# Scores of the latent queries: the product of query hi and key lo over 64 rows, two query tiles on two halves of TensorE's rows

## The chip, the cores and the metric

The kernel runs on one NeuronCore of one Trainium2 chip. The metric is the time of one execution on the device, in microseconds (us), as the median of several runs. TensorE does the matrix products into PSUM, VectorE (DVE), ScalarE (ACT) and GpSimd (POOL) do the rest, and SyncE issues the transfers (DMA).

## What is computed

Two layers of a diffusion block over 256 latent tokens and 256 context tokens of width 1024. Each layer normalises and modulates its input, projects it once, and runs three mixers on it: A, global attention; B, pooling; C, attention in a band of 128 tokens with a sink. A and C have 6 query heads and 2 key heads of 64 channels. The three are gated, summed and projected, and a squared-ReLU MLP follows. The part that the change touches is the scores, in the reference's words (A; C adds a mask and a sink):

```python
def one_block(qi):                       # 128 queries
    sc = jnp.einsum('bqhgd,bkhd->bhgqk', qi, k).astype(jnp.float32) * scale
    p = jax.nn.softmax(sc, axis=-1).astype(v.dtype)
    return jnp.einsum('bhgqk,bkhd->bqhgd', p, v)
```

Latent queries attend to the 256 context keys and 256 latent keys. Context queries attend to context keys alone, and only layer 0 needs them.

## The kernel before, in words

**Precision.** TensorE multiplies in a rounded fp32 format (fp32r). To keep fp32 accuracy each operand is split into a rounded part, hi, and the remainder, lo, and a product is the sum of three: hi·hi, hi·lo and lo·hi (`mm3`, line 439).

**Scores.** A head has only 64 channels, half of TensorE's 128 rows. So the query tile `q` (`Q`, lines 1162 to 1197) holds hi in one half of the rows and lo in the other: `Q.tile` writes hi and lo of each head side by side into a staging tile `stk` (line 1175), and `Q.finish` transposes it (TensorE, `qT`) and copies it to `q`. The keys (`KV`, lines 1113 to 1160) are staged twice over, so that `kh` holds key hi in both halves and `kl` holds key lo in both halves. `attend_unit` (lines 1208 to 1309) works on one head and one stream `s` (0 latents, 1 context), with two query tiles of 128. Per query tile it issues, over all 128 rows, `q` times `kh` (hi·hi + lo·hi) and `q` times `kl` (hi·lo + lo·lo). For latents (`lat`) each product has 512 columns (keys) and each query tile a PSUM bank of its own; in branch C a product of the identity and a mask, 128 columns, follows in the same bank. For context the products have 256 columns, and both query tiles share a bank. Then come the row maximum of each tile (VectorE, `mx`, line 1244), the exponential (ScalarE, `p`), the normalisation, the transposes of the probabilities (TensorE, `pT`), their split into hi and lo (`pth`, `ptl`) and the products with the values (`po`).

**Order.** All work is written as generators ("threads") with priorities, and `_Flow.run` (line 268) plays them against a simple model of the engines while the program is built: the thread that is ready in the model, with the lowest priority number, goes next. `_TensorEngine._step` (line 148) books 0.0022 us and one cycle for each column of a product, whatever its rows, and marks its output as ready 0.2 us later. Each engine then runs its instructions in the order that results. Attention units run as lanes (`attend_lane`, 2 per branch in layer 0, 3 in layer 1), and the projection, gate and branch products of the layer fill TensorE between their steps.

**A product with few rows elsewhere.** At the start `First.end` (line 546) turns rows of the modulation into columns with products over 4 rows of plain fp32 (`adat`, line 557), four per block, which appear as eight records each.

Of the kernel before, what the change touches and what calls it, by code (L numbers as in the profile page):

```python
# [15 lines left out]
P = 128  # L16
# [4 lines left out]
HD = 64  # L21
# [155 lines left out]
class _Flow:  # L177
# [58 lines left out]
    def free(self, *aps):  # L236

        for name in {ap.tensor.name for ap in aps}:
            self.shares[name] -= 1
            if self.shares[name]:  # L240
                continue
            p = self.pools[self.owner.pop(name)]
            p[0] -= 1
            p[1].append(self.uses[name] + 0.1)
# [48 lines left out]
P_NORM, P_ATT, P_SPLIT, P_SIDE, P_ADA, P_MAIN = range(6)  # L293
# [3 lines left out]
def kernel(ctx: ExitStack, tc: tile.TileContext, a: dict, out: bass.AP):  # L297
    nc = tc.nc
    ctx.enter_context(tc.manual_schedule())
    fl = _Flow()  # L300
# [3 lines left out]
    PE = _TensorEngine(fl, nc.tensor)  # L304
# [21 lines left out]
    def half(dt=F32, s="h"):  # L326
        t = bp.tile([P, 256], dt, tag="h", name=nm(s), bufs=T_BUFS)
        fl.take("h", t)
        return t

    def small(w, s="s", bufs=12):
        return sp.tile([P, w], F32, tag=s, name=nm(s), bufs=bufs)

    def bank(s="ps"):
        t = pp.tile([P, 512], F32, tag="ps", name=nm(s))
        fl.take("ps", t)
        return t
# [4 lines left out]
    def const(shape, dt, s):  # L342
        return cp.tile(shape, dt, tag=s, name=s)
# [367 lines left out]
    identr = const([P, P], F32R, "identr")  # L711
# [12 lines left out]
    mask = const([P, 2, P], F32R, "mask")  # L724
# [18 lines left out]
    def rms_scale(ss, n, width):  # L743

        V.tensor_scalar(out=ss, in0=ss, scalar1=1.0 / width, scalar2=EPS, op0=ALU.mult, op1=ALU.add)
        yield fl.ready(ss)
        G.tensor_tensor(out=ss, in0=ss, in1=neg_half[:, :n], op=ALU.pow)
# [159 lines left out]
    def layer(l, hT, hT_next):  # L907
# [35 lines left out]
        rsq = {br: cp.tile([P, 4, NH], F32, tag=f"rsq{br}", name=f"rsq{br}_{l}") for br in "AC"}  # L943

        def qk_norm(ps, c0, nh, kind, t, hi, lo, ev, rs=None):


            w = nh * HD
            src = ps[:, c0 : c0 + w]
            yield tabs_ev  # L950
            yield fl.ready(src)
            yield from fl.room("h", 2, T_BUFS)
            yield from S.calm(SIDE_CALM[l])
            sq = half(s="sq")
            rv = small(4, "qr")[:, :nh] if rs is None else rs
            if QR_ACT[l]:
                for i in range(nh):
                    S.activation(sq[:, i * HD : (i + 1) * HD], src[:, i * HD : (i + 1) * HD], AF.Square, accum_out=rv[:, i : i + 1])
            else:
                S.activation(sq[:, :w], src, AF.Square)  # L960
                yield fl.ready(sq[:, :w])
                V.tensor_reduce(out=rv, in_=sq[:, :w].rearrange("p (h d) -> p h d", h=nh), axis=AX.X, op=ALU.add)
            free(sq)
            zv = src.rearrange("p (h d) -> p h d", h=nh)
            z = None
            if rs is None:
                yield fl.ready(rv)
                yield from rms_scale(rv, nh, HD)
                yield fl.ready(rv)
                yield from fl.room("h", 1, T_BUFS)  # L970
                z = half(s="z")
                zn = z[:, :w].rearrange("p (h d) -> p h d", h=nh)
                V.tensor_tensor(out=zn, in0=zv, in1=rv.unsqueeze(2).to_broadcast([P, nh, HD]), op=ALU.mult)
                zv = zn
                yield fl.ready(z[:, :w])
            yield from fl.room("h", 3, T_BUFS)
            yield from V.calm(SIDE_CALM[l])
            y = half(s="y")
            yv = y[:, :w].rearrange("p (h d) -> p h d", h=nh)
            if t >= 2:  # L980
                V.tensor_tensor(out=yv, in0=zv, in1=gains[:, l, kind].unsqueeze(1).to_broadcast([P, nh, HD]), op=ALU.mult)
            else:
                y2 = y[:, :w].rearrange("p (h d e) -> p h d e", h=nh, e=2)
                ms = []
                for e in range(2):
                    m = half(s="m")
                    mv = m[:, :w].rearrange("p (h d) -> p h d", h=nh)
                    V.tensor_tensor(out=mv, in0=zv, in1=tabs[kind][:, e, t].unsqueeze(1).to_broadcast([P, nh, HD]), op=ALU.mult)
                    ms.append(m)
                yield fl.ready(*[m[:, :w] for m in ms])  # L990
                yield from V.calm(SIDE_CALM[l])
                for e in range(2):
                    m2 = ms[e][:, :w].rearrange("p (h d e) -> p h d e", h=nh, e=2)
                    V.tensor_tensor(out=y2[:, :, :, e], in0=m2[:, :, :, 0], in1=m2[:, :, :, 1], op=ALU.add)
                free(*ms)
            if z is not None:
                free(z)
            yield fl.ready(y[:, :w])
            if len(hi.shape) == 4:
                yv = yv.unsqueeze(2).to_broadcast([P, nh, 2, HD])  # L1000
            S.copy(out=hi.bitcast(F32R), in_=yv)
            yield fl.ready(hi)
            V.tensor_tensor(out=lo, in0=yv, in1=hi, op=ALU.subtract)
            free(y)
            fl.set(ev, lo)
            if rs is not None:
                V.tensor_scalar(out=rs, in0=rs, scalar1=HD * EPS, scalar2=None, op0=ALU.add)
                yield fl.ready(rs)
                G.tensor_tensor(out=rs, in0=rs, in1=neg_half[:, :nh], op=ALU.pow)
            done_with(ps)  # L1010
# [3 lines left out]
        def done_with(ps):  # L1014

            n = ps.tensor.name
            readers[n] -= 1
            if readers[n] == 0:
                free(ps)

        def reads(ps):
            readers[ps.tensor.name] = readers.get(ps.tensor.name, 0) + 1
# [90 lines left out]
        class KV:  # L1113
# [15 lines left out]
            def tile(self, t, ps):  # L1129
                st = tmp(s="stk").rearrange("p (h a e d) -> p h a e d", h=NKV, a=2, e=2)  # L1130
                self.sts.append(st)
                self.wait.append(_Event())
                reads(ps)
                reads(ps)
                fl.spawn(qk_norm(ps, 0, NKV, self.kind, t, st[:, :, 0], st[:, :, 1], self.wait[-1]), P_SIDE)
                fl.spawn(self.split_v(ps, t), P_SIDE)
# [25 lines left out]
        class Q:  # L1162
# [5 lines left out]
            def tile(self, t, ps):  # L1168
                st = tmp(s="stk").rearrange("p (h e d) -> p h e d", h=4, e=2)
                self.sts.append(st)  # L1170
                for c0, nh, kind, br, h0 in self.segs:
                    s = st[:, c0 // HD : c0 // HD + nh]
                    self.wait.append(_Event())
                    reads(ps)
                    fl.spawn(qk_norm(ps, c0, nh, kind, t, s[:, :, 0], s[:, :, 1], self.wait[-1], rsq[br][:, t, h0 : h0 + nh]), P_SIDE)

            def close(self):
                fl.spawn(self.finish(), P_SIDE)
# [29 lines left out]
        def attend_unit(br, h, s):  # L1208
# [5 lines left out]
            kh, kl = kkt[br, kv]  # L1214
            q = qst[br, h]
            lat = s == 0
            k0, nk = (0, 512) if lat else (256, 256)
            nb = nk // P
            mx = small(2, "mx")
            sc_ = []  # L1220
# [3 lines left out]
            for i in range(2):  # L1224
                qt = 2 * s + i
                qs = q[:, qt * P : (qt + 1) * P]
                sc = bank("sc") if lat else sc_bank[:, i * 256 : i * 256 + 256]
                masked = br == "C" and lat
                PE.matmul(sc[:, :nk], qs, kh[:, k0:], start=True, stop=False)
                PE.matmul(sc[:, :nk], qs, kl[:, k0:], start=False, stop=not masked)  # L1230
                if masked:
                    kb = 1 - qt
                    PE.matmul(sc[:, kb * P : (kb + 1) * P], identr, mask[:, qt], start=False, stop=True)
                sc_.append(sc)
            left[br, "q", h] -= 1
            if left[br, "q", h] == 0:
                free(q)
# [97 lines left out]
        def attend_lane(br, units):  # L1335
            for h, s in units:
                yield from attend_unit(br, h, s)
# [479 lines left out]
        for blk in range(nblk):  # L1817
# [63 lines left out]
            if blk == 0 and not last:  # L1881
# [3 lines left out]
                for j in range(2):  # L1885
                    w = ws.next()
                    w2_.append(w)
                    for i in range(2):
                        yield from banks()
                        ps = bank("h1")  # L1890
# [7 lines left out]
            if last:  # L1898
# [5 lines left out]
                for t in range(2):  # L1904
                    for j in range(2):
                        yield from banks()
                        ps = bank("h1")
# [11 lines left out]
            while c < nc1:  # L1919
                w = ws.next()  # L1920
                for i in range(2):
                    yield from banks()
                    ps = bank("h1")
# [46 lines left out]
    h0 = Normed()  # L1970
# [144 lines left out]
```

## Time and profile before

| what | us |
|---|---|
| median of 3 runs | 1152.64 |
| lowest and highest | 1149.83, 1153.02 |
| the profiled execution | 1151.59 |
| its span, first to last instruction | 1149.8 |
| its mean granted TensorE clock | 0.996 of 2.4 GHz |

How to read the rows further down: PE is TensorE's products, PEld its weight loads, which are instructions of their own in front of each product and run beside the product ahead. DVE is VectorE. `sc<-kk,q 128*128 128x512` is the product that writes `sc` from `kk` and `q`, with 128 rows by 128 columns of weights, and 128 x 512 of the other operand. L170 and L174 are the helper lines through which all products and transposes pass. Products are pipelined: the duration of one reaches from its start to the modelled end of its results, so products overlap in the timeline, and what one costs in a dense stream is the distance of the starts. A line that ends with a bracket tells of idle time before it and who ended it; "issue" there means that the engine waited for nothing that the profile shows.

### The profile page before, as it was taken

Reading aid. Unit: us, or ns where it says so; the run is one execution under the profiler, and the core shown is the slowest. Engines: PE = TensorE matmul, PEld = TensorE weight load, DVE = VectorE, ACT = ScalarE, POOL = GpSimd, SP = SyncE. Lnnn points to the kernel's source line nnn. Section 1 sums busy time; section 2 is a strip of 40 time slices with the busy share of each in tenths; the row PEclk is TensorE's granted clock in tenths of the full one; section 3 lists DMA queues with packets and bytes.
Section 4 is the critical chain, followed back from the end, with each engine's and each line's share of the span. In section 5 each row is a group of like instructions: output and inputs, shape, how many; then the busy total and the mean of one; then the engine's idle time right before and its main releaser. Section 6 shows DMA issues by size and latency. Waiting matters only on the chain.

```text
span 1149.8 us, 16635 instructions
## 1 busy us (share of the span) xinstructions
PE 1126.2 (98%) x5984; PEld 957.4 (83%) x5984; DVE 884.0 (77%) x1653; ACT 650.3 (57%) x1372; POOL 60.6 (5%) x76
## 2 busy tenths in 40 slices
PE   5999999999999999999999999999999999999998
PEld 2788888888888898888888888888888888999886
DVE  6889887899899679888676734679777886987453
ACT  7867668667653574422133423576878855765432
POOL 0123002000000100000000000012020000000000
PEclk9999999999999999999999999999999999999999
DMA  8742332353454335455555633555324570775662
GB/s 319 272 158 92 110 123 74 126 165 119 165 164 154 126 124 192 154 195 174 200 199 186 206 105 109 166 171 183 92 82 159 182 256 19 267 243 183 192 215 75
DMA packets 59987, 186.77 MB, mean 162 GB/s; under 512 B 7296, under 2 KB 8064, under 8 KB 59904
## 3 DMA queue, kind: packets, MB, share of 16 engines
q1 hardware_dynamic: 59904, 185.71, 48.7%
q8 instruction: 47, 0.77, 0.3%
q14 instruction: 36, 0.29, 0.1%
HBM read 184.63 MB, written 1.05 MB: 161 GB/s over the span
## 4 chain that ended last, share of the span: by engine, by line
PE 87%; DVE 6%; ACT 4%; DMA 2%; issue 1%; SPq 0%; POOL 0%; DVEq 0%; ACTq 0%
PE tm L170 28%; PE h L170 22%; PE g L170 15%; PE qkv L170 5%; PE br L170 4%; PE po L170 2%; PE sc L170 2%; PE pT L174 2%; DMA ad<-in_wada_dram 1%; PE u L170 1%; ACT hh L136 1%; PE ada L170 1%; PE xT L174 1%; ACT p L136 1%; DVE wl L136 1%
## 5 line engine op out<-in xcount | busy, mean ns | idle before, releaser
L136 DVE TENSOR_TENSOR wl<-st,wh 128x1024 fp32r<-128x1024 f32 x216 | 263.4, 1221 | 125.2 <-ACT wh L136 124.9
L136 ACT CAST wh<-st 128x1024 fp32r<-128x1024 f32 x216 | 227.8, 1058 | 223.5 <-PE tm L170 139.9
L170 PE MATMUL h<-hh,wh 128*128 128x256 f32 (+1 forms) x736 | 186.6, 316 | 0.0
L170 PE MATMUL h<-hh,wl 128*128 128x256 f32 (+1 forms) x512 | 168.8, 330 | 0.9 <-DVE wl L136 0.9
L136 DVE SCALAR_TENSOR_TENSOR acc<-sta,s_col,acc 128x512 f32<-128x512 f32 x224 | 159.3, 745 | 2.2 <-DMA sta<-in_wada_dram 1.8
L170 PE MATMUL tm<-wh,ah 128*128 128x512 f32 x384 | 149.9, 390 | 0.0
L170 PE MATMUL tm<-wl,ah 128*128 128x512 f32 x384 | 149.5, 389 | 0.0
L170 PE MATMUL tm<-wh,al 128*128 128x512 f32 x384 | 149.4, 389 | 0.0
L170 PEld LDWEIGHTS h<-hh,wh 128*128 128x128 f32 x736 | 124.3, 191 | 8.7
L170 PE MATMUL h<-hl,wh 128*128 128x512 f32 (+1 forms) x288 | 105.5, 366 | 0.1
L170 PEld LDWEIGHTS h<-hh,wl 128*128 128x128 f32 x512 | 97.3, 190 | 10.0 <-DVE wl L136 1.1
L170 PEld LDWEIGHTS tm<-wh,al 128*128 128x128 f32 x384 | 72.1, 188 | 15.2
L170 PEld LDWEIGHTS tm<-wl,ah 128*128 128x128 f32 x384 | 72.1, 188 | 14.9
L170 PEld LDWEIGHTS tm<-wh,ah 128*128 128x128 f32 x384 | 72.1, 188 | 14.6
L170 PE MATMUL g<-hh,wh 128*128 128x512 f32 x192 | 76.7, 400 | 0.0
L170 PE MATMUL g<-hh,wl 128*128 128x512 f32 x192 | 75.0, 391 | 0.0
L170 PE MATMUL g<-hl,wh 128*128 128x512 f32 x192 | 75.0, 391 | 0.0
L136 ACT ACTIVATE relu<-h 128x512 f32<-128x512 f32 (+1 forms) x64 | 31.0, 487 | 65.9 <-PE h L170 65.6
L170 PE MATMUL qkv<-wh,hh 128*128 128x256 f32 (+1 forms) x192 | 65.3, 340 | 1.1 <-ACT hh L136 1.1
L170 PE MATMUL qkv<-wl,hh 128*128 128x256 f32 (+1 forms) x192 | 64.3, 335 | 1.8 <-DVE wl L136 1.8
L170 PE MATMUL qkv<-wh,hl 128*128 128x256 f32 (+1 forms) x192 | 64.0, 333 | 0.0
L170 PEld LDWEIGHTS h<-hl,wh 128*128 128x128 f32 x288 | 54.3, 189 | 9.2 <-DVE hl L136 0.5
(207 smaller groups left out, 2230.9 us busy)
## 6 DMA issues: line engine op xcount, KB each, us to landing
st<-in_w_dram SPq DMA_DIRECT2D x136, 512.0 KB, 4.4
sta<-in_wada_dram SPq DMA_DIRECT2D x80, 512.0 KB, 4.0
st<-in_win_dram SPq DMA_DIRECT2D x48, 512.0 KB, 4.3
st<-in_wing_dram SPq DMA_DIRECT2D x24, 512.0 KB, 4.2
ad<-in_wada_dram SPq DMA_DIRECT2D x32, 256.0 KB, 6.1
st<-in_wout_dram SPq DMA_DIRECT2D x8, 512.0 KB, 4.7
wor<-in_wout_dram SPq DMA_DIRECT2D x16, 256.0 KB, 6.1
grow<-in_b_ada_dram SPq DMA_DIRECT2D x12, 256.0 KB, 5.5
```

What stands on the lines that cost most here:

```text
L136: return fn(*args, **kw)
L170: return self._e.matmul(out, lhsT, rhs, start=start, stop=stop)
L174: return self._e.transpose(out, in_, identity)
```

## The change

For latent units the two `q` times `kl` products over 128 rows are replaced. Now the two `kh` products (and in branch C the masks) of both query tiles come first, and then two products over 64 rows each: for query tile 0 the upper half of the rows, for query tile 1 the lower half, both of 512 columns, each into its tile's own bank. They hold hi·lo only, so lo·lo is no longer added. So that hi lies in the right half, `Q.tile` swaps hi and lo in the staging tile for odd query tiles. Context units keep their four products.

```diff
--- before.py
+++ after.py
@@ -1172,7 +1172,8 @@
                     s = st[:, c0 // HD : c0 // HD + nh]
                     self.wait.append(_Event())
                     reads(ps)
-                    fl.spawn(qk_norm(ps, c0, nh, kind, t, s[:, :, 0], s[:, :, 1], self.wait[-1], rsq[br][:, t, h0 : h0 + nh]), P_SIDE)
+
+                    fl.spawn(qk_norm(ps, c0, nh, kind, t, s[:, :, t % 2], s[:, :, 1 - t % 2], self.wait[-1], rsq[br][:, t, h0 : h0 + nh]), P_SIDE)
 
             def close(self):
                 fl.spawn(self.finish(), P_SIDE)
@@ -1227,11 +1228,16 @@
                 sc = bank("sc") if lat else sc_bank[:, i * 256 : i * 256 + 256]
                 masked = br == "C" and lat
                 PE.matmul(sc[:, :nk], qs, kh[:, k0:], start=True, stop=False)
-                PE.matmul(sc[:, :nk], qs, kl[:, k0:], start=False, stop=not masked)
+                if not lat:
+                    PE.matmul(sc[:, :nk], qs, kl[:, k0:], start=False, stop=True)
                 if masked:
                     kb = 1 - qt
-                    PE.matmul(sc[:, kb * P : (kb + 1) * P], identr, mask[:, qt], start=False, stop=True)
+                    PE.matmul(sc[:, kb * P : (kb + 1) * P], identr, mask[:, qt], start=False, stop=False)
                 sc_.append(sc)
+            if lat:
+                for i in range(2):
+                    r = slice(i * HD, i * HD + HD)
+                    PE.matmul(sc_[i], q[r, i * P : (i + 1) * P], kl[r], start=False, stop=True)
             left[br, "q", h] -= 1
             if left[br, "q", h] == 0:
                 free(q)
```

## Rows read from the trace of the kernel before

**Rows 1.** Page, busy us of each engine, share of the span.

```profile
PE 1126.2 (98%) x5984; PEld 957.4 (83%) x5984; DVE 884.0 (77%) x1653; ACT 650.3 (57%) x1372; POOL 60.6 (5%) x76
```

**Rows 2.** Page, the chain of work that ended last, by engine.

```profile
PE 87%; DVE 6%; ACT 4%; DMA 2%; issue 1%; SPq 0%; POOL 0%; DVEq 0%; ACTq 0%
```

**Rows 3.** Windows view: us, busy and count, granted clock; both attention stretches.

```profile
100.00:350.00 250.00, 249.42 (x1304) 211.66 (x1303) 220.68 (x452) 165.78 (x390) 10.39 (x9) 1.00 0.40 131
800.00:912.00 112.00, 109.64 (x612) 93.55 (x611) 89.47 (x198) 89.55 (x210) 6.21 (x6) 1.00 0.41 132
```

**Rows 4.** Waits of TensorE: us in total, times, longest.

```profile
PE po L170 <- DVE ptl L136: 0.9, 2, 0.7
...
PE pT L174 <- ACT p L136: 0.6, 2, 0.3
...
PE po L170 <- ACT p L136: 0.3, 1, 0.3
...
PE g L170 <- DVE wl L136: 0.2, 1, 0.2
```

**Rows 5.** Groups by form, score products: busy us, mean ns, idle before.

```profile
L170 PE MATMUL sc<-kk,q 128*128 128x512 f32 x96 | 27.7, 404 | 0.0
...
L170 PE MATMUL sc<-mask,identr 128*128 128x128 f32 x24 | 5.3, 221 | 0.0
```

**Rows 6.** Timeline, TensorE products, a steady stretch: start, us, what, [idle before].

```profile
274.80 0.39 PE L170 MATMUL br<-oh,kl 128*128 128x512 f32 x1
275.03 0.39 PE L170 MATMUL g<-hh,wh 128*128 128x512 f32 x1
275.25 0.39 PE L170 MATMUL g<-hl,wh 128*128 128x512 f32 x1
275.48 0.39 PE L170 MATMUL g<-hh,wl 128*128 128x512 f32 x1
```

**Rows 7.** Timeline, weight loads of the same stretch.

```profile
275.03 0.19 PEld L170 LDWEIGHTS g<-hl,wh 128*128 128x128 f32 x1
275.26 0.19 PEld L170 LDWEIGHTS g<-hh,wl 128*128 128x128 f32 x1
```

**Rows 8.** Timeline, products and loads at the start of one 4-row block.

```profile
45.82 0.60 PE L174 MATMUL xT<-ident,xh 128*128 128x128 f32 x4
...
46.35 0.18 PEld L170 LDWEIGHTS adat<-pair_sum,arow 4*128 4x128 f32 x1 [0.17 <-issue]
```

**Rows 9.** Timeline, the same at the start of another block.

```profile
44.14 0.28 PE L170 MATMUL qkv<-wh,hl 128*128 128x256 f32 x1
...
44.35 0.18 PEld L170 LDWEIGHTS adat<-pair_sum,arow 4*128 4x128 f32 x1
```

**Rows 10.** Timeline, products and loads at the end of the first block.

```profile
46.93 0.47 PE L170 MATMUL adat<-pair_sum,arow 4*128 4x2 f32 x3
...
47.33 0.19 PEld L170 LDWEIGHTS qkv<-wh,hh 128*128 128x128 f32 x1
```

**Rows 11.** Timeline, the same at the end of the other block.

```profile
44.93 0.47 PE L170 MATMUL adat<-pair_sum,arow 4*128 4x2 f32 x3
...
45.33 0.20 PEld L174 LDWEIGHTS xT<-ident,xh 128*128 128x128 f32 x2
```

**Rows 12.** Timeline, the loads of the whole first block.

```profile
46.35 0.96 PEld L170 LDWEIGHTS adat<-pair_sum,arow 4*128 4x128 f32 x8 [0.17 <-issue]
```

**Rows 13.** Timeline, the last product of a latent unit of branch C.

```profile
270.42 0.22 PE L170 MATMUL sc<-mask,identr 128*128 128x128 f32 x1
```

**Rows 14.** Waits of VectorE, the row maxima: us, times, longest.

```profile
DVE mx L136 <- PE sc L170: 20.5, 17, 4.1
```

**Rows 15.** Timeline, the weight load behind the product of rows 13.

```profile
270.42 0.14 PEld L174 LDWEIGHTS pT<-ident,p 128*128 128x128 f32 x1
```

## The prediction

> **What bounds the kernel now.** I read the page's busy shares first, then its chain of work, then the stretches in which the attention runs, then single instructions around the products that change. TensorE is busy for 1126.2 of 1149.8 us and holds 87% of the chain that ended last [rows 1, 2]. In the two attention stretches it is busy for 249.4 of 250 and 109.6 of 112 us, at a granted clock of 1.00 (2.4 GHz), while VectorE has 29 and 22 us to spare [rows 3]. All that TensorE waits for in the attention's own products, and in the gate products run among them, is a few waits of under 1 us in sum each [rows 4]. So the end moves with the time that TensorE's instruction stream takes, and with hardly anything else. One run beside another can tell 0.3% (3.5 us) from no change.
>
> **What the change touches.** There are 96 score products of 512 columns [rows 5]: 24 latent units (2 layers, 2 branches, 6 heads), four each. In each unit the two "query times key lo" products over 128 rows go, and two over 64 rows come, one on the upper and one on the lower half of the rows, one behind the other at the end of the unit. The swap of the halves for odd query tiles only alters which half of a staging tile is written: the same two instructions per tile, no cost. The mask products of branch C stay, ahead of the new pair. No DMA, no other instruction and no queue changes.
>
> **Price of a product as it is.** A 512-column product shows 0.39 us, but starts follow each other by 0.23 us (274.80, 275.03, 275.25, 275.48) [rows 6], since the weights of the next are loaded while one streams: each load starts with the product before its own [rows 7]. So the pair costs 2 × 0.23 = 0.46 us now. Laid fully over each other, two products would cost 0.23: a gain of 0.23 us a unit, 24 × 0.23 = 5.5 us. That is all that can be gained.
>
> **Price of changing the row mode.** The trace has one kind of product that doesn't fill the rows: the 4-row products of the modulation's start (adat), in blocks of eight records. At both edges of a block the overlap of load and product is gone. Before one block the last 128-row product ends at 45.82 + 0.60 = 46.42, and the first 4-row load starts at 46.35, 0.07 us before that end, with 0.17 us of idleness put down to "issue", so to no wait that the profile shows [rows 8]; another block is entered alike (44.14 + 0.28 = 44.42, load at 44.35) [rows 9]. On the way out it is the same: 46.93 + 0.47 = 47.40 and 44.93 + 0.47 = 45.40, with loads at 47.33 and 45.33 [rows 10, 11]. Inside a block loads follow each other by (0.96 - 0.19) / 7 = 0.11 us [rows 12], so there the load is not held. I read this as: a load of another row mode starts only 0.07 us before the modelled end of the product ahead, and its product streams 0.11 us later.
>
> The Trainium skill, "TensorEngine Tiling (Array Packing)", Key Properties, says that changing the tiling mode, though not the tile, drains TensorE. By that rule, the trace agrees at these four edges with its 0.07 us; a 64-row edge is in no row here.
>
> *Entry.* In branch A the product ahead is one of 512 columns (0.39 us), starting at S. The load starts at S + 0.32, its product streams at S + 0.43 instead of S + 0.23: 0.20 us lost. In branch C it is a mask product (0.22 us) [rows 13], after which the next product is held by its own load to S + 0.11 anyway: now S + 0.15 + 0.11 = S + 0.26, so 0.15 us lost. *Exit.* The second 64-row product is one of 512 columns: 0.20 us lost, whatever follows. Bounds: a gain is not excluded if half-array modes cost no drain (0 per switch); above, nothing in the rows is dearer than 0.20.
>
> *The pair itself.* Below: both loads run together and both products stream together, gain 0.23. Above: the products don't overlap, gain 0. Between: the second load follows the first by 0.11 us as in the 4-row block, and its product streams 0.11 us behind the first, gain 0.23 - 0.11 = 0.12. I take the last, because the 4-row loads are the nearest row, though they all use the same rows of the array.
>
> The same skill, "TensorE: Matmul & The Clock Gate", Part 3, gives about 4 ns between the starts of packed products on different row groups; no row here shows such a pair. By it the gain would be 0.23 us, and the sum worked out below 3.5 us instead of 6.1.
>
> **What follows on the other engines.** The first row maximum of a unit now waits for the fourth or sixth product instead of the second or third. Counted from the start of the second hi product: before, the first lo product ended at 0.39 - 0.23 = 0.16; now the pair's first ends at 0.43 + 0.39 = 0.82, 0.66 us later, while TensorE's own next work is 0.28 later. Queued behind the maximum on VectorE are weight splits and modulation sums. That is up to 0.38 × 24 = 9.1 us more of waiting, on an engine with 51 us to spare in these stretches, besides the 20.5 us which the maxima wait already [rows 3, 14]. I cost it at nothing: the order written by the planner books both lo products ahead of the maximum (2 × 0.2155 us by its own price), so it already moves the transposes back by most of that. If that cover is gone, TensorE stalls at the probability transposes. The planner's new order may also change the waits of these stretches, of which TensorE has 0.6 + 2.4 us now: I allow ±2 us.
>
> **The sum.** Branch A: 0.20 + 0.20 - 0.12 = 0.28 us a unit; branch C: 0.15 + 0.20 - 0.12 = 0.23. Twelve units each: 3.4 + 2.8, about 6.1 us longer. The profiled execution took 1151.59 us, so 1157.7; the median shown is 1.05 above it, which would give 1158.7. I put the forecast between them, at 1158.
>
> **Rivals.**
> - *Half modes cost no drain* (faster). The four edges [rows 8 to 11] are of products of plain fp32 and a quarter of the rows, and the drain may belong to that. Against: the transposes are declared fp32 too, and their load starts with the product ahead (270.42 on both engines) [rows 13, 15]. The edge at the unit's end decides: below about 0.12 us per switch (half of 0.23) the change gains. With none, 24 × 0.23 = 5.5 us go: 1146 to 1147. Chance 0.24.
> - *Drain, but loads and products wholly together.* Branch A 0.40 - 0.23 = 0.17, branch C 0.12: 12 × 0.29 = 3.5 us, 1155 to 1156, at the edge of what is told from no change. This is the case of the Trainium skill's page on the clock gate, cited above. Chance 0.16.
> - *Drain and no overlap: the change doesn't do what it says.* 0.40 and 0.35: 9.0 us, about 1161. For it: every product in the trace streams after the one ahead. Chance 0.13.
> - *Stalls at the transposes on top of the forecast.* If half of the 0.38 us reached TensorE, 4.6 us more: 1162 to 1163. Against: the waits of TensorE for the maxima's successors are 1.8 us in all now [rows 4]. Chance 0.07.
>
> **How the numbers follow.** My forecast (drain at both edges, loads in turn) has 0.40. Its own range is 1155 to 1161 (±2 of the order, ±1 of the median). For 8 in 10, I go from 1147, the upper end of the no-drain case, to 1162; that leaves out half of the no-drain case (0.12) and most of the stalls (0.05). Faster by over 0.3%: the no-drain case but for a sixth of it, where the order gives back some of its 5.5 us, 0.20. Within 0.3%: that sixth (0.04), half of the 0.16 and a fifth of my 0.40, where the order helps by its 2 us and more, in all 0.20. Slower: what is left, 0.60.
>
> **What the changed profile would show.** Right: score products listed with 64 rows, 48 of them; the first load of each pair 0.07 us before the end of the product ahead, and the load behind the pair likewise; the second load 0.11 us after the first, and the second product starting before the first has streamed; TensorE's idle time before "sc" and its successors up by some 0.4 us a unit, most of it "issue". Wrong: a load of the pair starting with the last 128-row product, as in rows 7 (no drain); both loads together (3.5 us); second product 0.23 us or more behind the first (9.0 us); new waits of pT or po for VectorE or ScalarE (stalls).

## The result, and the profile after

The changed kernel takes 1171.41 us (median of 4 runs, 1170.68 to 1172.92), the kernel before 1151.28: a ratio of 1.0173, with an interval of 1.016 to 1.0186. It is 20 us slower. I had forecast slower, but 6 us, and had ended the range at 1162.

The page of the changed kernel, its span, busy shares and clock, against [rows 1]:

```profile
span 1169.1 us, 16655 instructions
...
PE 1135.8 (97%) x5984; PEld 955.9 (82%) x5984; DVE 884.1 (76%) x1653; ACT 651.4 (56%) x1372; POOL 61.3 (5%) x76
...
PEclk9999999989999999999999999999899999999999
```

The span grew by 19.3 us: TensorE's busy time by 9.6, its idle time by 9.7 (33.3 against 1149.8 - 1126.2 = 23.6). The other engines do the same work as before. Two slices of the clock stand at 8, near 250 and 830 us; before, all were at 9.

The pair itself in the timeline: the weight loads of one unit of branch A (first fence), the products of one unit of branch C (second fence), with what stands ahead and behind:

```profile
151.85 0.31 PEld L170 LDWEIGHTS sc<-kk,q 128*128 128x128 f32 x2
152.53 0.19 PEld L170 LDWEIGHTS sc<-kk,q 64*128 64x128 f32 x2 [0.37 <-issue]
152.96 0.19 PEld L170 LDWEIGHTS g<-hh,wh 128*128 128x128 f32 x1 [0.24 <-issue]
153.07 0.19 PEld L170 LDWEIGHTS g<-hl,wh 128*128 128x128 f32 x1
```

```profile
296.36 0.22 PE L170 MATMUL sc<-mask,identr 128*128 128x128 f32 x1
296.51 0.50 PE L170 MATMUL sc<-kk,q 64*128 64x512 f32 x2
296.94 0.50 PE L170 MATMUL g<-hh,wh 128*128 128x512 f32 x1
297.27 0.39 PE L170 MATMUL g<-hl,wh 128*128 128x512 f32 x1
```

Both drains are there, as at the edges of the 4-row block [rows 8 to 11], that is, the next weight load waits until the product ahead is all but through: the load of the pair starts at 296.51, 0.07 us before the mask product's end at 296.36 + 0.22, and the load behind the pair 0.07 us before the pair's end, 296.51 + 0.50 (its product is listed with it, at 296.94). But the two loads of a pair take 0.19 us together, as long as one alone, and two products of 0.50 us end within 0.50 us: they run side by side from the first column. That was my second rival. In branch C the next product streams at 297.27 - 0.23 = 297.04, 0.68 us after the mask product's start, where two products and the mask's own 0.11 took 0.57: 0.11 us lost, twelve times. In branch A the product ahead started at 152.53 - 0.32 = 152.21 and the one behind the pair streams at 153.07, 0.86 us later, where three products took 0.69: 0.17 us lost, twelve times. Together 12 × 0.28 = 3.4 us, an estimate from these two units.

The rest is in the waits of TensorE, against [rows 4]:

```profile
PE po L170 <- DVE ptl L136: 4.4, 2, 3.0
PE yT L174 <- DVE y L136: 2.6, 2, 2.4
...
PE g L170 <- DVE o L136: 1.6, 1, 1.6
PE po L170 <- ACT pth L136: 1.4, 1, 1.4
PE pT L174 <- ACT p L136: 1.3, 3, 0.7
...
PE po L170 <- DVE t L136: 1.2, 1, 1.2
```

These are new stalls at single places. The largest, TensorE's timeline and then VectorE's in the same stretch:

```profile
250.51 1.42 PE L174 MATMUL pT<-ident,p 128*128 128x128 f32 x11 [0.28 <-ACT p L136]
251.77 0.60 PE L174 MATMUL act<-ident,fold 128*128 128x128 f32 x4
253.73 0.38 PE L170 MATMUL po<-pth,v 128*128 128x256 f32 x1 [1.36 <-ACT pth L136]
257.10 0.58 PE L170 MATMUL po<-ptl,v 128*128 128x256 f32 x1 [2.98 <-DVE ptl L136]
```

```profile
251.37 1.41 DVE L136 SCALAR_TENSOR_TENSOR acc<-sta,s_col,acc 128x512 f32<-128x512 f32 x2
252.70 1.22 DVE L136 TENSOR_TENSOR wl<-st,wh 128x1024 fp32r<-128x1024 f32 x1
253.83 0.69 DVE L136 TENSOR_TENSOR kl<-kr,kh 128x512 fp32r<-128x512 f32 x1
254.43 1.41 DVE L136 SCALAR_TENSOR_TENSOR acc<-sta,s_col,acc 128x512 f32<-128x512 f32 x2
255.76 0.69 DVE L136 TENSOR_REDUCE mod<-act 128x8 f32<-128x512 f32 x1
256.36 1.28 DVE L136 TENSOR_TENSOR ptl<-pT,pth 128x512 fp32r<-128x512 f32 x2
```

On TensorE the value products stand directly behind the transposes of the probabilities and four short transposes of the modulation, with no long product between, and on VectorE the split that they need (`ptl`) stands behind 5 us of sums and weight splits. In the kernel before, branch products stand between the last transposes and the value products near here, and `po` doesn't wait (TensorE's timeline before):

```profile
249.68 0.60 PE L174 MATMUL pT<-ident,p 128*128 128x128 f32 x4
250.03 0.71 PE L170 MATMUL br<-oh,kh 128*128 128x512 f32 x2
250.58 0.40 PE L170 MATMUL br<-oh,kl 128*128 128x512 f32 x1
250.81 0.28 PE L170 MATMUL po<-pth,v 128*128 128x256 f32 x1
```

VectorE's work takes as long as before (884.1 against 884.0 us); it stands in another order. And the stalls have a second price. The windows view (us, busy of PE, PEld, DVE, ACT and POOL, then the granted clock) of three stretches around this stall, and of two behind the stall of `po` near 830 us:

```profile
247.00:255.50 8.50, 4.77 (x27) 3.45 (x25) 8.43 (x16) 8.17 (x18) 0.00 (x0) 0.98 0.57 188
255.60:262.30 6.70, 5.20 (x21) 4.34 (x22) 4.69 (x10) 0.63 (x2) 0.00 (x0) 0.53 0.54 192
262.50:270.00 7.50, 7.50 (x36) 6.11 (x35) 7.38 (x18) 5.95 (x14) 0.00 (x0) 1.00 0.23 70
832.50:839.20 6.70, 6.70 (x24) 4.71 (x24) 3.45 (x7) 3.83 (x8) 0.00 (x0) 0.53 0.26 79
839.40:846.00 6.60, 6.60 (x41) 5.52 (x40) 6.09 (x13) 5.69 (x14) 0.00 (x0) 1.00 0.00 0
```

TensorE stood for 3.7 of 8.5 us. In the next stretch it was granted 0.53, nearly all of it the lower of its two levels (1.2 GHz), and behind that 2.4 GHz again. Near 832 us it is the same. Between 100 and 1140 us of the kernel before the granted clock is 1.00 throughout. By estimate, work of 5.2 and 6.7 busy us at 0.53 costs 0.47 of that, 5.6 us.

So of 19.3 us, 9.7 are idle, some 5.6 slower clock and 3.4 the pair, 18.7 in all. The clock's part is gross. Both kernels also have two stretches at 0.50 in their first 51 us, with 8.8 busy us before and 6.4 after; that gives back about 1.2 us, and leaves some 1.8 us of the 19.3 unexplained.

### The profile page after: what moved, and what is told of

Read it like the earlier page. It is cut to its first block, busy times and chain, and to the rows that moved or that the text cites. A ratio compares the mean times of both kernels' runs of the same rounds, so it can differ in the third digit from the quotient of the medians.

```text
span 1169.1 us, 16655 instructions
## 1 busy us (share of the span) xinstructions
PE 1135.8 (97%) x5984; PEld 955.9 (82%) x5984; DVE 884.1 (76%) x1653; ACT 651.4 (56%) x1372; POOL 61.3 (5%) x76
## 4 chain that ended last, share of the span: by engine, by line
PE 89%; ACT 4%; DVE 4%; DMA 2%; issue 1%; SPq 0%; POOL 0%; DVEq 0%; ACTq 0%
PE tm L170 28%; PE h L170 22%; PE g L170 15%; PE qkv L170 7%; PE br L170 5%; PE po L170 2%; PE sc L170 2%; PE pT L174 2%; PE u L170 1%; DMA ad<-in_wada_dram 1%; ACT hh L136 1%; ACT p L136 1%; DVE wl L136 1%; PE xT L174 1%; PE qT L174 1%
```

## The experiments

**Order against pair.** While the program is built, the planner books each product and records when its output is ready. In a latent unit nothing else is booked between the products, and their sum is the same in both kernels. What differs afterwards is in the main one number: the first tile's scores count as ready one product (0.0022 + 512 / 2400 = 0.22 us, where the planner counts the full clock) later, in branch C one mask more. From there on the orders of all engines part. That this number is the cause is read from the code; the runs show that what the planner is told is the cause. `old_order_64` books the products in the order of before and issues the pair as the change does (`emit=False` books without issuing, `book=False` the reverse):

```diff
+                PE.matmul(sc[:, :nk], qs, kh[:, k0:], emit=False)
+                PE.matmul(sc[:, :nk], qs, kl[:, k0:], emit=False)
-                PE.matmul(sc[:, :nk], qs, kh[:, k0:], start=True, stop=False)
+                PE.matmul(sc[:, :nk], qs, kh[:, k0:], start=True, stop=False, book=False)
...
                     r = slice(i * HD, i * HD + HD)
-                    PE.matmul(sc_[i], q[r, i * P : (i + 1) * P], kl[r], start=False, stop=True)
+                    PE.matmul(sc_[i], q[r, i * P : (i + 1) * P], kl[r], start=False, stop=True, book=False)
```

> The pair of 64-row products as in the changed kernel, but the planner is told of the products of before, so that every other instruction of every engine stands in the order of before. Theory 1 (the pair itself costs 0.17 us a unit in branch A and 0.12 in branch C, as read from the changed trace, and the rest of the 20 us comes from the new order of the other work): 3.5 us over the kernel before, some 1154 to 1156, no stall of po over 1 us. Theory 2 (the row modes and the later row maxima stall the engines whatever the order): 10 to 20 us over the kernel before, with po or pT waiting.

Measured: 1154.51 us, ratio 1.0024 (1.0014 to 1.0034), 3.0 us over the kernel before. Its page, its score products, the longest waits in its attention and VectorE's wait for the scores (waits views):

```profile
PE 1128.6 (98%) x5984; PEld 950.2 (82%) x5984; DVE 883.9 (77%) x1653; ACT 650.2 (56%) x1372; POOL 60.0 (5%) x76
...
PEclk9999999999999999999999999999999999999999
```

```profile
L170 PE MATMUL sc<-kk,q 64*128 64x512 f32 x48 | 12.0, 497 | 0.0
```

```profile
PE po L170 <- DVE ptl L136: 0.7, 2, 0.5
PE pT L174 <- ACT p L136: 0.5, 2, 0.3
...
DVE mx L136 <- PE sc L170: 26.3, 20, 4.6
```

All 48 products over 64 rows are there, the stalls are not. Theory 1 holds, with its number. The row maxima do wait 5.8 us longer in all (26.3 against 20.5 [rows 14]), and it doesn't reach TensorE. In the traces the instructions of TensorE (score products apart), VectorE, ScalarE and GpSimd stand in one and the same order in this kernel and in the kernel before, by tiles and shapes. In the changed kernel 788 of VectorE's 1653 places hold another instruction.

The reverse, `new_order_128`: the changed kernel with its order, the last two products over all rows.

```diff
-                    r = slice(i * HD, i * HD + HD)
-                    PE.matmul(sc_[i], q[r, i * P : (i + 1) * P], kl[r], start=False, stop=True)
+                    PE.matmul(sc_[i], q[:, i * P : (i + 1) * P], kl, start=False, stop=True)
```

> The order of the changed kernel in all engines, but the last two products of a latent unit over all 128 rows, as before the change. Theory 1 (new order of the other work): 3.5 us less than the changed kernel and no more, some 1166 to 1169, with the waits of po near 252 and 830 us still there. Theory 2 (row modes): back to the kernel before, 1150 to 1153.

Measured: 1171.67 us, ratio 1.0168 (1.0148 to 1.0188). By the traces its order is that of the changed kernel on all four engines. No product over 64 rows is left, and the loss is all there, with the same stalls at the same places (timeline of TensorE, three places; 2.98 and 2.42 as in the changed kernel, 1.51 against 1.6):

```profile
251.32 0.38 PE L170 MATMUL po<-pth,v 128*128 128x256 f32 x1 [1.36 <-ACT pth L136]
254.68 0.51 PE L170 MATMUL po<-ptl,v 128*128 128x256 f32 x1 [2.98 <-DVE ptl L136]
...
913.51 0.78 PE L170 MATMUL g<-wh,hh 128*128 128x512 f32 x1 [1.51 <-DVE o L136]
...
949.29 0.30 PE L174 MATMUL yT<-ident,y 128*128 128x128 f32 x1 [2.42 <-DVE y L136]
```

I had expected 1166 to 1169, the changed kernel less the pair's 3.5 us. The median doesn't show these, and the interval is as wide as that. The clock is a reason for the width: in the profiled execution four stalls (near 255, 828, 914 and 951 us) are followed by a stretch at 0.50, where the changed kernel's has two, and the five runs spread from 1167.24 us at a mean granted clock of 0.993 to 1173.27 at 0.986. Runs at the same granted clock can be compared: at 0.993 it is 1167.24 against 1170.68 and 1171.98 of the changed kernel, at 0.991 it is 1169.41 against 1170.84 and 1172.92. That is 1.4 to 4.7 us for the pair, in line with its 3 us, but from two runs.

**The later row maxima.** `old_order_128_late` is `old_order_64` with the two last products over all 128 rows: only the place of the lo products in the unit is new.

```diff
-                    r = slice(i * HD, i * HD + HD)
-                    PE.matmul(sc_[i], q[r, i * P : (i + 1) * P], kl[r], start=False, stop=True, book=False)
+                    PE.matmul(sc_[i], q[:, i * P : (i + 1) * P], kl, start=False, stop=True, book=False)
```

> Order of all other work as before, all products over 128 rows, but inside a latent unit the two lo products come last. Theory 1: nothing on the path waits for the maxima, within 1 us of the kernel before. Theory 2 (the later maxima stall VectorE and then TensorE): 3 us or more over the kernel before.

Measured: 1151.87 us, ratio 1.0006 (0.9997 to 1.0015). Issuing the lo products late costs nothing that can be measured; telling the planner of it (`new_order_128`) costs 20 us.

**Which half.** `old_order_64_same_half` puts query hi of both tiles into the upper half (of the first changed line only the two arguments are shown).

```diff
-s[:, :, t % 2], s[:, :, 1 - t % 2]
+s[:, :, 0], s[:, :, 1]
...
-                    r = slice(i * HD, i * HD + HD)
+                    r = slice(0, HD)
```

> As old_order_64, but query hi of both tiles lies in the upper half, so that both 64-row products use the same half of the rows. If the pair runs side by side on the two halves: the second product starts 0.23 us behind the first here, 24 times 0.23 us, 5 to 6 us over old_order_64. If the halves give nothing: the same time as old_order_64.

Measured: 1159.24 us, ratio 1.0066 (1.0052 to 1.008), 4.7 us over `old_order_64`, or 0.20 us a unit, a little under what was expected.

**A second pair.** `old_order_64_twice` issues each pair again before the mode is left; query hi times key lo is thus added twice.

```diff
+                    PE.matmul(sc_[i], q[r, i * P : (i + 1) * P], kl[r], start=False, stop=False, book=False)
+                for i in range(2):
+                    r = slice(i * HD, i * HD + HD)
                     PE.matmul(sc_[i], q[r, i * P : (i + 1) * P], kl[r], start=False, stop=True, book=False)
```

> As old_order_64, but each pair of 64-row products is issued a second time right behind the first, without leaving the row mode (so query hi times key lo is added twice). If entering and leaving the mode is what the pair pays, and inside it two products go side by side: 0.22 to 0.23 us a unit more, 24 times that, 5 to 6 us over old_order_64. If each pair pays a drain of its own: 0.4 us a unit, 9 to 10 us over old_order_64. If the two products of a pair are not really side by side: 0.45 us a unit, 11 us.

Measured: 1158.68 us, ratio 1.0064 (1.0043 to 1.0085), 4.2 us over `old_order_64`, or 3.5 (by the medians) to 4.6 (by the ratios) when each is set against the kernel before that was run beside it. That is again a little under, and far from 9 to 11. Weight loads in the timeline, first of the same-half kernel, then of the one with two pairs, both in branch A:

```profile
152.16 0.29 PEld L170 LDWEIGHTS sc<-kk,q 64*128 64x128 f32 x2 [0.36 <-issue]
152.82 0.42 PEld L174 LDWEIGHTS pT<-ident,p 128*128 128x128 f32 x4 [0.37 <-issue]
```

```profile
150.79 0.30 PEld L170 LDWEIGHTS sc<-kk,q 64*128 64x128 f32 x4 [0.36 <-issue]
151.46 0.20 PEld L174 LDWEIGHTS pT<-ident,p 128*128 128x128 f32 x2 [0.37 <-issue]
```

From the first load of the pair to the load behind it: 0.43 us in the changed kernel (152.53 to 152.96), 0.66 with both on one half, 0.67 with two pairs. On one half the loads come about 0.1 us apart (0.29 - 0.19) and the second product streams 0.23 us later, on two halves both at once; a second pair adds 0.24 us and no drain. So the halves do what the change says. What a unit pays is the way in and out.

**Where the order costs.** The 64-row pair in both layers, the new order told in one layer only (here layer 0; the other kernel has `l == 0` in the first line; the products issued are then booked where `old` is false, which is not shown):

```diff
+                old = not lat or l == 1
+                if old:
+                    PE.matmul(sc[:, :nk], qs, kh[:, k0:], emit=False)
+                    PE.matmul(sc[:, :nk], qs, kl[:, k0:], emit=False)
```

> The 64-row pair in both layers; the planner is told of the new order of the products in layer 0, of the old one in layer 1. If the loss sits in the stalls that the new order brings, layer 0's part (the stall of po near 252 us and the half clock behind it, some 8 to 9 us) is here: 1160 to 1166, and no new stall after 800 us. If the pair is dear wherever it stands: 1171, or 1154.5 if the order is not the cause at all.

> The reverse: the new order told in layer 1 alone. Layer 1's part of the loss (stalls of po near 830, of g near 917 and of yT near 950 us, and one stretch of half clock, some 8 to 10 us) is here: 1160 to 1166, with no stall of po near 252 us. The two layers' losses over old_order_64 add up to that of the changed kernel, 16 to 17 us.

Measured: 1166.48 us (1.0134) and 1159.69 us (1.0072), which is 12.0 and 5.2 us over `old_order_64`; together 17.2, against the 16.9 of the changed kernel. The losses add up, as expected, though each is just outside its range, and they are not at the places expected. With the new order in layer 0 alone, layer 1 has the stall of `po` too (timeline, both places):

```profile
254.44 0.39 PE L170 MATMUL po<-pth,v 128*128 128x256 f32 x1 [1.36 <-ACT pth L136]
257.80 0.58 PE L170 MATMUL po<-ptl,v 128*128 128x256 f32 x1 [2.98 <-DVE ptl L136]
...
831.66 0.38 PE L170 MATMUL po<-pth,v 128*128 128x256 f32 x1 [1.22 <-DVE t L136]
833.45 0.39 PE L170 MATMUL po<-ptl,v 128*128 128x256 f32 x1 [1.41 <-DVE ptl L136]
```

So what the planner is told in one layer moves the order of the next. With the new order in layer 1 alone there is no stall of `po` near 252 us, but the stalls expected after 800 us are missing or shorter too: none of `g` for VectorE's `o`, and these two are the longest of their kinds (waits view of `new_order_layer1_only`):

```profile
PE po L170 <- DVE ptl L136: 1.4, 2, 1.0
PE yT L174 <- DVE y L136: 1.3, 2, 0.8
```

So the long stall of `po` after 800 us comes with the order told in layer 0, and those of `g` and `yT` reach their full length only with both. That the two losses add up to that of the changed kernel is thus in part chance.

**Is it this order, or any other?** One constant of the planner is changed, no product: `PV_SLACK` in the kernel before (`before_replanned`) and `ATT_SLACK` in the changed one (`after_replanned`).

```diff
-PV_SLACK = (0.3, 0.5)
+PV_SLACK = (0.2, 0.5)
-ATT_SLACK = (0.2, 0.5)
+ATT_SLACK = (0.1, 0.5)
```

> The kernel before, with no change to any product: one constant of the planner, the slack ahead of the value products in layer 0, is 0.2 instead of 0.3 us. If the order of before is one that few others match, any new order costs: 3 to 10 us over the kernel before, with new stalls. If the loss comes from the later row maxima alone, and the order matters little otherwise: within 2 us of the kernel before.

> The changed kernel with another constant of the planner, the slack ahead of the probability transposes in layer 0, 0.1 instead of 0.2 us. If the order makes the loss, another order gives another loss: 3 us or more away from the changed kernel, in either direction, probably down to 1160 to 1168. If the pair or its position makes it: within 2 us of the changed kernel, 1171.

Measured: 1160.56 us, ratio 1.0084 (1.0069 to 1.0099), 9.3 us over the kernel before; and 1166.3 us, ratio 1.0125 (1.0109 to 1.014), 5.1 us under the changed kernel. The kernel before, replanned, has stalls of its own (waits view):

```profile
PE pT L174 <- ACT p L136: 2.8, 4, 1.9
...
PE tm L170 <- DVE yh L136: 1.6, 2, 1.1
```

A step of 0.1 us in one slack loses nearly half of what the change lost, with the same products on the same engines. Of the five other orders tried here none is as good as that of before; the nearest, new in layer 1 alone, is 5.2 us worse.

## Why the prediction was wrong

- *What bounds the kernel* was right: TensorE's stream, and so every stall in it, sets the end.
- *The price of changing the row mode* was right: 0.07 us before the modelled end at each edge, as at the 4-row block. "TensorEngine Tiling (Array Packing)" of the Trainium skill, Key Properties, says drain, and the 64-row edges of this trace agree with their 0.07 us. (I called those products a quarter of the rows; the rows show 4 of 128.)
- *The pair itself* was mis-sized. I took the loads in turn, gain 0.12 us, from loads that use the same rows; they start together, gain 0.23. My 6.1 us should have been 3.5, and 3.0 were measured in `old_order_64`. "TensorE: Matmul & The Clock Gate" of the Trainium skill, Part 3, gives about 4 ns between the starts of such products; the rows above agree, with 0.19 us for both loads and 0.50 us for both products. The rival "drain, but loads and products wholly together" was the right one for the pair, at 0.16.
- *The step that failed* is "the planner's new order may also change the waits of these stretches [...] I allow ±2 us". The order cost 17 of the 20 us (1171.41 against 1154.51). I had read this bound from TensorE's present waits, 0.6 + 2.4 us, as if they showed what an order can do. They showed what this one order does. A bound from both sides had to ask how many orders are as good, which the rows of one order can't tell; nothing excluded 10 us and more.
- In the same place, I said that the planner books both lo products ahead of the first maximum. It books one product more than before, 0.22 us: the first maximum waits for the third product in branch A and the fifth in branch C, not for the fourth or sixth. The later maximum itself is hidden, as I had costed it (`old_order_128_late`).
- *Stalls at the transposes*, my last rival, named the right kind of place (successors of the maxima on TensorE) but the wrong cause: the stalls stay when no drain is left, and go when the order of before is kept. Of the clock I had said only that it stood at 1.00; that a stall would be followed by a stretch at the lower level was not in the sum.
- That the direction came out right owes little to my sum. The pair alone, which was all that the sum priced, cost 3.0 us, inside the 3.5 us that I had called no change.

## What to carry to other kernels

Where a planner writes the order of all engines, a local edit is two edits: the instructions, and what the planner is told. Price them apart, and run them apart: the old order with the new instructions, and the new order with the old ones. The good order of a tuned kernel need not tell anything of its neighbours; without runs of a few of them, the range needs room on the slow side, here 10 to 20 us. And a change of the row mode pays in and out once: one overlapped pair of 512 columns (0.23 us gained) doesn't cover 0.35 to 0.40 us.

Not tried: the pairs of two units in one stay in the mode (0.40 - 2 × 0.23 = -0.06 us for two units of branch A, by the numbers above, an estimate), and a search for a better order of the changed kernel. No run here beats the kernel before.

## What the runs showed of the hardware

Two weight loads for different halves of the rows take the time of one (0.19 us for both), while two for the same half come about 0.1 us apart. Leaving and entering the 64-row mode looks alike at all edges: the next load starts 0.07 us before the modelled end of the product ahead. And two stalls of `po` (1.36 + 2.98 us, and 1.22 + 1.41 us) were each followed by a stretch at a granted clock of 0.53, that is at the lower level for nearly all of it, which by estimate cost 2.4 and 3.1 us more (0.47 × 5.2 and 0.47 × 6.7 busy us). It doesn't follow every stall: behind the waits of `g` (1.6 us) and `yT` (2.4 us) the changed kernel's profile has 1.00, that of `new_order_128`, with the same order, 0.50.
